# mLSTM head 3: a written instruction order for its backward recursion, later masks and output gate, and one root stage for heads 2 and 3

## The chip, the cores and the metric

The kernel runs on one NeuronCore of a Trainium2 chip. TensorE (PE) does the matrix products, VectorE (DVE), ScalarE (ACT) and GpSimd (POOL) the elementwise work, and SyncE (SP) issues the DMA transfers. The metric is the device time of one launch in microseconds, lower is better; the median of several runs is compared.

## The reference, cut to what matters

The reference is one layer of a hybrid backbone: a modulated RMSNorm, one input projection, a bidirectional mLSTM with 4 heads of 128 channels beside a windowed attention, an output projection with a gated residual, and a convolutional GLU. The part that the change touches is the mLSTM of the last head and the merge behind it:

```python
def step(carry, inp):                       # one chunk of the recursion
    c_st, n_st, m_st = carry
    c_l, n_l, m_l, bt = inp
    m_new = jnp.maximum(bt + m_st, m_l)
    a = jnp.exp(bt + m_st - m_new)
    s = jnp.exp(m_l - m_new)
    return (a * c_st + s * c_l, a * n_st + s * n_l, m_new), (c_st, n_st, m_st)
...
def mlstm_merge(h, o, gain):
    hn = h * lax.rsqrt(jnp.mean(h * h, axis=-1, keepdims=True) + EPS)
    hn = hn.transpose(0, 2, 1, 3).reshape(b, l, MLSTM_W) * gain
    return (hn * jax.nn.sigmoid(o)).astype(o.dtype)
```

The recursion runs once forward and once backward over the chunks. Within a chunk a decay matrix with a triangular mask weights the products of queries and keys. The sum of both directions is divided by its root mean square over the head's channels, multiplied by a gain and by a sigmoid of the gate `o`.

## The kernel before, in words

The sequence of 1024 latent tokens and 256 context tokens is cut in chunks of 128 (8 latent, 2 context). The heads are worked one after the other. While head h runs its recursion, PE also computes dense projections that belong to something else: for heads 0 to 2 the keys, queries, values and gates of head h+1; for head 3 the attention queries (`qgen`, 16 projections `px` in groups of six matmuls with 256 columns each, which VectorE rotates by L319 and L320). The loop at the end of the head section takes one step of `mlstm(h)` and then as many pieces of the dense work as a rate (`RATE3` = 0.37 us a step for head 3) allows. The steps of `mlstm` are numbered n here:

- n = 0 and 1: PE transposes the first two chunks of keys (L653, into PSUM tile `pn`), ScalarE makes the two weighted copies `kwb` (L657) and `kwf` (L659).
- n = 2 to 10: the backward recursion, i = 0 to 8. Each step transposes the keys of two chunks ahead, multiplies (L680), and VectorE adds the product to the decayed state (L688 for the first, L690 after that). In the same steps stand: the loads of the decay matrices `ee` (L647, first three steps), one step of the finish of the head before (`fins`), `mask(i - 2)` (L663, VectorE), `decay` of a chunk (L667, two exponentials on ScalarE), and at i = 7 the output gate (L703 Tanh on ScalarE over 128x1024, L704 on VectorE).
- n = 11 and 12: two steps of the forward recursion over the context chunks (L710, L713, L715), with the last mask and two decays.
- n = 13 to 29: the latent chunks. `first` multiplies queries and keys (L722) and takes a forward step (L710), and VectorE weights the product with the decay (L725). `second` makes the outputs (L733, L734, L736), ScalarE and VectorE combine and divide them (L739 to L748), and L751 sums the squares in `hss`. `decay(5)` to `decay(7)` are in this part.
- finish: a root of `hss` (L784), a reciprocal (L785) and eight products of hidden value, reciprocal and gate, one for a chunk (L787). For heads 0 to 2 this is spread over the recursion of the next head; for head 3 it comes at once at the end.

What sets the order of instructions: inside a `manual_schedule` block, the engines named there run their instructions in the order in which they are written. For the other engines a planner orders them, from its own cost estimates, by what it takes to be ready and by how early they are written. For heads 0 to 2, PE, VectorE, ScalarE, GpSimd and SyncE are all in written order. For head 3 PE alone is; VectorE, ScalarE and SyncE are planned. The instructions of two blocks, or of a block and of the planned code around it, can interleave on an engine.

`pn`, `pe`, `pj`, `pi` and the transposes of the attention queries share four PSUM buffers (pool `pl`), so the transpose of step i waits until VectorE has read the product of the step four tiles before. [...]

At n = 12 (`LW3`) the loop calls `late()`: it loads the second half of the query weights in two DMA transfers through one buffer, and casts and splits each (L156 ScalarE, L157 VectorE). After head 3 the memory of the mLSTM is released, and tiles for the attention (`wm`: `kT2`, `vv`, rows of the output weight) are placed there. The table of Exp is then brought in by L1032. The attention stage and the GLU stage behind it are in written order on PE, VectorE, ScalarE and GpSimd.

Of the kernel before, what the change touches and what calls it, by code (L numbers as in the profile page):

```python
# [12 lines left out]
AF = mybir.ActivationFunctionType  # L13
ALU = mybir.AluOpType
# [4 lines left out]
P = 128  # L19
# [4 lines left out]
NL = SEQ // P  # L24
NC = CTX // P
NCH = NL + NC
H = 4
# [21 lines left out]
TN = 7  # L49
# [29 lines left out]
def build(tc, I, out, dbg=None):  # L79
# [550 lines left out]
        if h == 0:  # L630
            dump("kT", kT[:]); dump("qT", qT[:]); dump("va", va[:].rearrange("p c e -> p (c e)"))

    fins = []

    def mlstm(h, kT, qT, va):
        cbk = tp.tile([P, NL, DH + 1], F32, name="cbk", tag="cbk", bufs=1)
        kwf = tp.tile([P, NCH - 1, DH], F32, name="kwf", tag="kwf", bufs=1)
        hid = tp.tile([P, NL, DH], F32, name="hid", tag="hid", bufs=1)
        hss = tp.tile([P, NL], F32, name="hss", tag="hss")
        g1 = lambda t, d, c: t[:, d, c, h:h + 1]  # L640
        yv = ym[:, :, h * DH:(h + 1) * DH]
        E1 = DH + 1


        ee = tp.tile([P, NL, 2, P], F32, name="ee", tag="ee", bufs=1)
        def ee_load(b):
            nc.sync.dma_start(ee[:, b:b + 2], m_d[:].rearrange("(c h) d t -> h c d t", h=H)  # L647
                              [h:h + 1, NC + b:NC + b + 2].broadcast_to([P, 2, 2, P]))

        ee_load(0)  # L650
        def tr(c):
            pn = pl.tile([P, 512], F32, name="pn", tag="l")
            T.transpose(pn[:, 0:P], kT[:, c * P:(c + 1) * P], ident[:])  # L653
            kwb = None
            if c != NC:
                kwb = tp.tile([P, DH], F32, name="kwb", tag="kwb", bufs=3)
                S.activation(kwb[:], pn[:, 0:P], AF.Copy, scale=g1(gw, 1, c))  # L657
            if c < NCH - 1:
                S.activation(kwf[:, c], pn[:, 0:P], AF.Copy, scale=g1(gw, 0, c))  # L659
            return pn, kwb  # L660

        def mask(b):
            V.tensor_tensor(out=ee[:, b], in0=ee[:, b], in1=tri[:], op=ALU.add)  # L663

        def decay(b):
            for d in range(2):
                S.activation(ee[:, b, d], ee[:, b, d], AF.Exp, bias=g1(a_, d, NC + b), scale=-1.0)  # L667

        ahead = [tr(order[1][0])]
        yield  # L670
        ahead.append(tr(order[1][1]))
        yield
        prev = None
        for i, c in enumerate(order[1][:-1]):
            pn, kwb = ahead.pop(0)
            if i + 2 < NCH - 1:
                ahead.append(tr(order[1][i + 2]))
            elif i + 2 == NCH - 1:
                tr(order[1][i + 2])
            T.matmul(pn[:, P:P + E1], kwb[:], va[:, c], start=True, stop=True)  # L680
            if c == 1:
                nx = tp.tile([P, E1], F32, name="cst", tag="cst")[:]
            elif c == 0:
                nx = cbk[:, NL - 1]
            else:
                nx = cbk[:, c - NC - 1]
            if prev is None:
                V.tensor_copy(nx, pn[:, P:P + E1])  # L688
            else:
                V.scalar_tensor_tensor(out=nx, in0=prev, scalar=g1(gd, 1, c), in1=pn[:, P:P + E1],  # L690
                                       op0=ALU.mult, op1=ALU.add)
            prev = nx
            if i < 3:
                ee_load(2 * i + 2)
            if fins and i:
                next(fins[0])
            if i > 1:
                mask(i - 2)
            if i in (4, 6, 8):
                decay(i // 2 - 2)  # L700
            if i == TN:

                S.activation(yv, yv, AF.Tanh, scale=0.5)  # L703
                V.scalar_tensor_tensor(out=yv, in0=yv, scalar=1.0, in1=rwc("gain", h * DH, DH).unsqueeze(1)  # L704
                                       .broadcast_to([P, NL, DH]), op0=ALU.add, op1=ALU.mult)
            yield
        cf, cfs = [None], []

        def step(c, ps):
            T.matmul(ps, kwf[:, c], va[:, c], start=True, stop=True)  # L710
            nx = tp.tile([P, E1], F32, name="cst", tag="cst")
            if cf[0] is None:
                V.tensor_copy(nx[:], ps)  # L713
            else:
                V.scalar_tensor_tensor(out=nx[:], in0=cf[0], scalar=g1(gd, 0, c), in1=ps, op0=ALU.mult, op1=ALU.add)  # L715
            cf[0] = nx[:]
            cfs.append(nx[:])

        def first(c):
            b = c - NC  # L720
            pe = pl.tile([P, 512], F32, name="pe", tag="l")
            T.matmul(pe[:, 0:P], kT[:, c * P:(c + 1) * P], qT[:, b * P:(b + 1) * P], start=True, stop=True)  # L722
            if b:
                step(c - 1, pe[:, P:P + E1])
            V.scalar_tensor_tensor(out=ee[:, b], in0=pe[:, 0:P].unsqueeze(1).broadcast_to([P, 2, P]),  # L725
                                   scalar=float(DH) ** -0.5, in1=ee[:, b], op0=ALU.mult, op1=ALU.mult)

        def second(c):
            b = c - NC
            qs = qT[:, b * P:(b + 1) * P]  # L730
            pj = pl.tile([P, 512], F32, name="pj", tag="l")
            pi = pl.tile([P, 512], F32, name="pi", tag="l")
            T.matmul(pj[:, 0:E1], qs, cfs.pop(0), start=True, stop=True)  # L733
            T.matmul(pj[:, E1:2 * E1], qs, cbk[:, b], start=True, stop=True)  # L734
            for d in range(2):
                T.matmul(pi[:, d * E1:(d + 1) * E1], ee[:, b, d], va[:, c], start=True, stop=True)  # L736
            nm = tp.tile([P, 2, E1], F32, name="nm", tag="nm")
            for d in range(2):
                S.activation(nm[:, d], pj[:, d * E1:(d + 1) * E1], AF.Copy, scale=g1(gi, d, c))  # L739
            V.tensor_tensor(out=nm[:], in0=pi[:, 0:2 * E1].rearrange("p (d e) -> p d e", d=2), in1=nm[:], op=ALU.add)  # L740
            dn = tp.tile([P, 2], F32, name="dn", tag="dn")
            V.scalar_tensor_tensor(out=dn[:], in0=nm[:, :, DH], scalar=-1.0, in1=nm[:, :, DH], op0=ALU.mult, op1=ALU.max)
            V.tensor_tensor(out=dn[:], in0=dn[:], in1=gfl[:, :, c, h], op=ALU.max)
            V.reciprocal(dn[:], dn[:])

            def rest():
                S.activation(hid[:, b], nm[:, 0, 0:DH], AF.Copy, scale=dn[:, 0:1])
                V.scalar_tensor_tensor(out=hid[:, b], in0=nm[:, 1, 0:DH], scalar=dn[:, 1:2], in1=hid[:, b],  # L748
                                       op0=ALU.mult, op1=ALU.add)
                yield  # L750
                S.activation(nm[:, 0, 0:DH], hid[:, b], AF.Square, accum_out=hss[:, b:b + 1])  # L751
                yield
            return rest()

        for c in range(NC):
            pn = pl.tile([P, 512], F32, name="pn", tag="l")
            step(c, pn[:, 0:E1])
            if c == 0:
                cfs.clear()
            if c == 0:  # L760
                mask(NL - 1)
            decay(3 + c)
            yield
        first(NC)
        tail = None
        yield
        for c in range(NC, NCH):
            if c + 1 < NCH:
                first(c + 1)
            if tail:  # L770
                next(tail)
            yield
            if c < NC + 3:
                decay(5 + c - NC)
            if tail:
                next(tail)
            tail = second(c)
            yield
        for _ in tail:
            pass  # L780
        cfs.clear()

        def finish():
            S.activation(hss[:], hss[:], AF.Sqrt, bias=eps_t[:], scale=1.0 / DH)  # L784
            V.reciprocal(hss[:], hss[:])  # L785
            for b in range(NL):
                V.scalar_tensor_tensor(out=yv[:, b], in0=hid[:, b], scalar=hss[:, b:b + 1], in1=yv[:, b],  # L787
                                       op0=ALU.mult, op1=ALU.mult)
                if b < NL - 1:
                    yield  # L790
            fins.clear()
            yield
        if h < H - 1:
            fins.append(finish())
        else:
            for _ in finish():
                pass

    def ada_second():
        R4 = 4 * KT
# [172 lines left out]
    for h in range(H):  # L977
# [20 lines left out]
        with tc.manual_schedule(engines=order_):  # L998
            dn = dense(h + 1, wkq, wvo, *nh) if nh else qgen()
            rate = RATE if nh else RATE3  # L1000
            for n, _ in enumerate(mlstm(h, *cur)):
                if nh is None and n == LW3:
                    late()
                    rga = pq.tile([P, D], F32, name="rga", tag="rga")
                    nc.sync.dma_start(rga[:], row(0))
# [1177 lines left out]
```

## Time and profile before

| | us |
|---|---|
| median of 3 runs | 1265.78 (1265.62 to 1266.16) |
| time of the profiled execution | 1265.89 |
| its span (first to last instruction) | 1264.1 |
| head 3: first transpose to last product of the last chunk | 322.2 to 354.2 |
| first score of the attention stage | 394.5 |

The granted TensorE clock is 0.998 of full speed. In the profile, a row of a timeline gives start, length, engine, line, operation and tiles, and in brackets the idle time of the engine before it with what ended it. A row of windows gives the busy time of each engine in a stretch with the number of its instructions. A row of the waits gives the engine and line that waited, for whom, the total, the number of times and the longest.

### The profile page before, as it was taken

What the parts mean: (1) busy time and instruction counts of PE and PEld (TensorE: products, weight loads), DVE (VectorE), ACT (ScalarE), POOL (GpSimd) and SP (SyncE); (2) the same over time, 40 slices, a digit from 0 to 9 for tenths busy, and PEclk for the clock granted to TensorE, in tenths of its full rate; (3) what the DMA queues carried; (4) which work ended last, traced back from release to release, by engine and by line L of the source; (5) the groups of instructions that cost most, each with busy time, mean ns of one, the idle gap of its engine ahead of it and who ended that gap; (6) DMA issues with size and microseconds to landing.
All of it is one profiled execution on the core that took longest, in us unless ns stands there. A gap on an engine that the chain in (4) does not pass through costs nothing.

```text
span 1264.1 us, 19253 instructions
## 1 busy us (share of the span) xinstructions
PE 1234.4 (98%) x7047; PEld 1060.2 (84%) x7047; DVE 972.8 (77%) x1691; ACT 637.9 (50%) x1309; POOL 187.1 (15%) x162
## 2 busy tenths in 40 slices
PE   6999999999999999999999999999999999999997
PEld 4799999999898888888887888888888888788886
DVE  5873777777787888788987877777777777877887
ACT  6632556464865777776843333333333334434435
POOL 1200000000001443221002232133231232001000
PEclk9999999999999999999999999999999999999999
DMA  9541535362354333104313322223322237975553
GB/s 361 184 142 34 145 115 153 115 181 75 85 175 160 134 120 115 51 34 167 117 51 130 115 99 102 95 102 117 103 105 100 93 135 269 335 250 187 195 192 134
DMA packets 90560, 176.17 MB, mean 139 GB/s; under 512 B 12954, under 2 KB 29538, under 8 KB 90466
## 3 DMA queue, kind: packets, MB, share of 16 engines
q1 hardware_dynamic: 90178, 174.15, 41.2%
q8 instruction: 56, 0.92, 0.3%
q10 hardware_dynamic: 288, 0.79, 0.2%
q14 instruction: 38, 0.31, 0.1%
HBM read 136.58 MB, written 38.33 MB: 138 GB/s over the span
## 4 chain that ended last, share of the span: by engine, by line
PE 84%; DVE 6%; ACT 5%; DMA 3%; issue 2%; POOL 1%; SPq 0%; ACTq 0%; DVEq 0%; POOLq 0%
PE pd L2020 14%; PE pa L1480 8%; PE pc L1480 8%; PE pp L588 7%; PE pe L1480 4%; PE pd L1480 4%; PE pb L1480 4%; PE u L1182 3%; PE pv L307 2%; PE pv L309 2%; PE pv L308 2%; PE po L307 2%; PE po L309 2%; PE po L308 2%; PE pt L1159 2%
## 5 line engine op out<-in xcount | busy, mean ns | idle before, releaser
L1597 ACT CAST wh<-Rb 128x1024 fp32r<-128x1024 f32 (+1 forms) x63 | 56.8, 903 | 144.1 <-PE pd L1480 77.1
L2020 PE MATMUL pd<-dh,al 128*128 128x512 f32 x296 | 115.4, 390 | 0.9 <-DVE al L1361 0.9
L2020 PE MATMUL pd<-dl,ah 128*128 128x512 f32 x296 | 115.3, 389 | 0.0
L2020 PE MATMUL pd<-dh,ah 128*128 128x512 f32 x296 | 115.1, 389 | 0.0
L1480 PE MATMUL pc<-hB,wh 128*128 128x512 f32 x344 | 105.6, 389 | 0.0
L1480 PE MATMUL pa<-hB,wh 128*128 128x512 f32 x336 | 103.8, 390 | 0.2 <-ACT sn L1679 0.2
L1198 DVE TENSOR_TENSOR wl<-Rb,wh 128x1024 fp32r<-128x1024 f32 (+1 forms) x63 | 65.8, 1045 | 39.2 <-ACT wh L1597 38.6
L1715 POOL TENSOR_TENSOR tt<-vt,tt 128x512 f32<-128x512 f32 x22 | 29.5, 1341 | 367.5 <-ACT tt L1709 367.5
L588 PE MATMUL pp<-hl,wh 128*128 128x512 f32 x256 | 79.3, 405 | 0.0
L307 PE MATMUL pv<-wh,hl 128*128 128x256 f32 x256 | 75.9, 296 | 0.0
L1480 PEld LDWEIGHTS pc<-hB,wh 128*128 128x128 f32 x344 | 64.6, 188 | 13.5
L1480 PEld LDWEIGHTS pa<-hB,wh 128*128 128x128 f32 x336 | 62.9, 188 | 14.1 <-ACT sn L1679 1.1
L309 PE MATMUL pv<-wh,hl 128*128 128x256 f32 x256 | 72.4, 283 | 0.0
L308 PE MATMUL pv<-wl,hl 128*128 128x256 f32 x256 | 72.3, 282 | 0.0
L2020 PEld LDWEIGHTS pd<-dh,al 128*128 128x128 f32 x296 | 55.6, 188 | 13.1 <-DVE al L1361 1.6
L1480 PE MATMUL pc<-hB,wl 128*128 128x512 f32 x172 | 66.4, 389 | 0.0
L2020 PEld LDWEIGHTS pd<-dl,ah 128*128 128x128 f32 x296 | 55.5, 188 | 11.8 <-DVE dl L1361 0.3
L1480 PE MATMUL pa<-hB,wl 128*128 128x512 f32 x168 | 65.4, 389 | 0.0
L2020 PEld LDWEIGHTS pd<-dh,ah 128*128 128x128 f32 x296 | 55.6, 188 | 11.6
L1166 ACT CAST ph<-pt 128x512 fp32r<-128x512 f32 (+1 forms) x88 | 46.2, 525 | 25.3 <-PE pt L1159 25.0
L1136 DVE TENSOR_REDUCE nm<-sps 128x1 f32<-128x641 f32 (+1 forms) x64 | 50.3, 786 | 4.9 <-PE sps L1132 3.4
L1480 PE MATMUL pd<-hB,wh 128*128 128x512 f32 x176 | 54.0, 390 | 0.0
(1082 smaller groups left out, 3694.4 us busy)
## 6 DMA issues: line engine op xcount, KB each, us to landing
w<-in_w_ada_dram SPq DMA_DIRECT2D x64, 256.0 KB, 2.8
br<-in_w_down_dram SPq DMA_DIRECT2D x25, 512.0 KB, 5.9
ar<-act_s SPq DMA_DIRECT2D x44, 256.0 KB, 4.0
Ra<-in_w_up_dram SPq DMA_DIRECT2D x21, 512.0 KB, 3.6
Rb<-in_w_up_dram SPq DMA_DIRECT2D x21, 512.0 KB, 3.6
act_a<-tt SPq DMA_DIRECT2D x33, 256.0 KB, 2.0
act_s<-tt SPq DMA_DIRECT2D x33, 256.0 KB, 2.0
wr<-in_w_h_dram SPq DMA_DIRECT2D x16, 512.0 KB, 4.1
```

The costliest lines, as they stand in the source:

```text
L307: T.matmul(ps, st_hi, mv_hi, start=first, stop=False)
L308: T.matmul(ps, st_hi, mv_lo, start=False, stop=False)
L309: T.matmul(ps, st_lo, mv_hi, start=False, stop=last)
L588: T.matmul(pp[:, 512 * n:512 * n + 512], wkq[sw][:, kt, cs], hl[n][part][:, kt, :], start=kt == 0 and sw + part == 0, stop=kt == KT - 1 an ...
L1136: V.tensor_reduce(out=self.nm[:, j:j + 1], in_=self.sv[j], axis=AX.X, op=ALU.max, negate=True)
L1166: S.copy(self.ph[i][:, :w], self.pt[i][:, :w])
L1182: T.matmul(self.u[:], vv[:, c, self.g], part[i][:, kk * 2 * P:(kk + 1) * 2 * P], start=kb + m == 0, stop=kb == last and m == 1)
L1198: sub = lambda e, o, x, y: e.tensor_tensor(out=o, in0=x, in1=y, op=ALU.subtract)
L1480: T.matmul(ps[:, cols], wt[sw][:, j, kt * P:kt * P + P], hB[part][:, blk, kt, cols], start=first and n == 0, stop=last and n == len(seq) - ...
L1597: S.copy(wt[0][:], src)
L1715: G.tensor_tensor(out=self.tt[:, h2_], in0=self.vt[:], in1=self.tt[:, h2_], op=ALU.mult)
L2020: T.matmul(ps[:], ac[sa][:, js], w[sw], start=first and n == 0, stop=last and n == 2, skip_group_check=not fresh)
```

## The change

Seven edits, all for the mLSTM:

1. For head 3, VectorE, ScalarE and GpSimd too are put in written order, from the start of head 3 to n = 13; the block is left there. SyncE stays planned.
2. `late_` = 2 for head 3: in the backward recursion, `mask(i - 4)` takes the place of `mask(i - 2)`, so five masks and two decays are there in place of seven and three. The other masks and decays follow one by one at n = 11, 12 and 13; `decay(5)` to `decay(7)` stay where they were.
3. The output gate of head 3 leaves step i = 7 and comes behind the squares of chunk b = 2, in the second half of the head (n = 21), where the planner orders.
4. The finish of head 2, inside head 3's recursion, is one product of 128x1024 (hidden value by gate) at i = 1 in place of a root, a reciprocal and eight products. It needs no root.
5. At the end of head 3: one such product for head 3, then two roots, then two reciprocals, then two products of 128x1024 with the reciprocal broadcast along the channels (heads 2 and 3).
6. The Sqrt table is thus brought in once for heads 2 and 3, at the end.
7. `late()` moves from n = 12 to n = 13, behind the end of the block.

```diff
-            if i > 1:
-                mask(i - 2)
-            if i in (4, 6, 8):
-                decay(i // 2 - 2)
-            if i == TN:
-
-                S.activation(yv, yv, AF.Tanh, scale=0.5)
-                V.scalar_tensor_tensor(out=yv, in0=yv, scalar=1.0, in1=rwc("gain", h * DH, DH)...
+            if i > 1 + late_:
+                mask(i - 2 - late_)
+            if i in (4 + late_, 6 + late_, 8):
+                decay((i - late_) // 2 - 2)
+            if i == TN and not late_:
+                gate()
...
                 S.activation(nm[:, 0, 0:DH], hid[:, b], AF.Square, accum_out=hss[:, b:b + 1])
+                if late_ and b == 2:
+                    gate()
...
-            if c == 0:
-                mask(NL - 1)
-            decay(3 + c)
+            if late_:
+                mask(5 + c)
+                decay(2 + c)
+            else:
+                if c == 0:
+                    mask(NL - 1)
+                decay(3 + c)
             yield
         first(NC)
+        if late_:
+            mask(NL - 1)
+            decay(4)
...
+        def gated():
+            V.tensor_tensor(out=yv, in0=hid[:], in1=yv, op=ALU.mult)
+            held.append((hss, yv))
+            fins.clear()
+            yield
-        if h < H - 1:
+        if h < H - 2:
             fins.append(finish())
+        elif h < H - 1:
+            fins.append(gated())
         else:
-            for _ in finish():
+            for _ in gated():
                 pass
+            for s_, _ in held:
+                S.activation(s_[:], s_[:], AF.Sqrt, bias=eps_t[:], scale=1.0 / DH)
+            for s_, _ in held:
+                V.reciprocal(s_[:], s_[:])
+            for s_, y_ in held:
+                V.tensor_tensor(out=y_, in0=y_, in1=s_[:].unsqueeze(2).broadcast_to([P, NL, DH]), op=ALU.mult)
...
+            if nh is None:
+                inner = tc.manual_schedule(engines={mybir.EngineType.DVE, mybir.EngineType.Activation, mybir.EngineType.Pool})
+                inner.__enter__()
             for n, _ in enumerate(mlstm(h, *cur)):
-                if nh is None and n == LW3:
+                if nh is None and n == LW3 + 1:
+                    inner.__exit__(None, None, None)
                     late()
```

`gate()` is a new function that holds the two instructions removed above (L703 and L704).

More of the change, by code (lines that the diff above doesn't have):

```diff
@@ L631, in dense @@
             dump("kT", kT[:]); dump("qT", qT[:]); dump("va", va[:].rearrange("p c e -> p (c e)"))
-    fins = []
+    fins, held = [], []
     def mlstm(h, kT, qT, va):
@@ L667, in decay, with gate @@
                 S.activation(ee[:, b, d], ee[:, b, d], AF.Exp, bias=g1(a_, d, NC + b), scale=-1.0)
+        def gate():
+            S.activation(yv, yv, AF.Tanh, scale=0.5)
+            V.scalar_tensor_tensor(out=yv, in0=yv, scalar=1.0, in1=rwc("gain", h * DH, DH).unsqueeze(1)
+                                   .broadcast_to([P, NL, DH]), op0=ALU.add, op1=ALU.mult)
+        late_ = 2 if h == H - 1 else 0
         ahead = [tr(order[1][0])]
@@ L696, in mlstm @@
                 next(fins[0])
-            if i > 1:
-                mask(i - 2)
-            if i in (4, 6, 8):
-                decay(i // 2 - 2)
-            if i == TN:
-                S.activation(yv, yv, AF.Tanh, scale=0.5)
-                V.scalar_tensor_tensor(out=yv, in0=yv, scalar=1.0, in1=rwc("gain", h * DH, DH).unsqueeze(1)
-                                       .broadcast_to([P, NL, DH]), op0=ALU.add, op1=ALU.mult)
+            if i > 1 + late_:
[4 more added lines that the diff above has]
+                gate()
             yield
```

## The prediction

> **What bounds the kernel now.** The order of reading was: the page for the span, the windows over head 3 for where PE loses time, the waits for what ended its idle time, the timeline of PE, and last the groups of VectorE and ScalarE in the stretch where PE waits.
>
> ```profile
> span 1264.1 us, 19253 instructions
> ```
>
> The profiled execution took 1265.89 us, 1.8 us more than this span, and lies 0.11 us over the median of 1265.78 us. The sum below is made against 1265.89.
>
> The windows give, from left, PE, weight loads, VectorE, ScalarE and GpSimd:
>
> ```profile
> 325.00:330.00 5.00, 3.85 (x29) 3.10 (x27) 4.43 (x13) 4.26 (x13) 0.00 (x0) 1.00 0.96 173
> 330.00:335.00 5.00, 4.19 (x33) 3.61 (x32) 5.00 (x19) 4.97 (x16) 0.00 (x0) 1.00 0.20 70
> 335.00:340.00 5.00, 5.00 (x46) 5.00 (x46) 4.96 (x14) 4.75 (x15) 0.00 (x0) 1.00 0.18 59
> 340.00:345.00 5.00, 5.00 (x46) 5.00 (x45) 4.53 (x17) 3.43 (x11) 0.00 (x0) 1.00 0.15 54
> 345.00:350.00 5.00, 4.21 (x37) 4.05 (x36) 4.74 (x23) 3.39 (x14) 0.00 (x0) 1.00 0.26 102
> 350.00:355.00 5.00, 5.00 (x46) 5.00 (x46) 3.76 (x17) 4.18 (x15) 0.00 (x0) 1.00 0.14 52
> ```
>
> Between 325 and 335 PE starts 62 matmuls, against 46 in five microseconds where it runs full. VectorE and ScalarE are nearly full there, so they are what PE waits for. The second thing to see is VectorE at 4.5 to 5.0 of 5 until 350: behind the recursion there is little room on it.
>
> ```profile
> PE pj L733 <- DVE ee L725: 0.8, 1, 0.8
> PE pn L653 <- DVE cst L688: 0.7, 1, 0.7
> ...
> PE pn L680 <- ACT kwf L659: 0.6, 2, 0.4
> ```
>
> These are PE's largest waits in head 3. Busy time understates the loss, because the end of a pipelined matmul is modelled; the starts show it better:
>
> ```profile
> 324.89 0.27 PE L653 MATMUL pn<-ident,kT 128*128 128x128 f32 x1
> 325.36 0.49 PE L680 MATMUL pn<-va,kwb 128*128 128x129 f32 x2 [0.20 <-ACT kwf L659]
> 326.57 0.33 PE L653 MATMUL pn<-ident,kT 128*128 128x128 f32 x1 [0.73 <-DVE cst L688]
> ...
> 327.68 0.28 PE L653 MATMUL pn<-ident,kT 128*128 128x128 f32 x1
> 327.79 0.39 PE L680 MATMUL pn<-va,kwb 128*128 128x129 f32 x2
> 327.93 0.36 PE L307 MATMUL px<-wh,hl 128*128 128x256 f32 x1
> ...
> 333.88 0.39 PE L710 MATMUL pn<-va,kwf 128*128 128x129 f32 x2
> ...
> 335.76 0.61 PE L722 MATMUL pe<-qT,kT 128*128 128x128 f32 x4
> ```
>
> The stretch from the transpose of step n = 3 (324.89) to the first forward step (333.88) takes 8.99 us. Unhindered, a transpose takes 0.11 us from start to start (327.68 to 327.79), a product 0.14 (327.79 to 327.93), and two forward steps, each a product and a group of six projection matmuls, 1.88 (333.88 to 335.76), which leaves 0.80 for a group. Steps n = 3 to 10 hold seven transposes, eight products and four groups: 0.77 + 1.12 + 3.20 = 5.09 us. PE loses **3.9 us** here. That is the most that this stretch can give.
>
> **What VectorE and ScalarE do meanwhile,** from 323.9 to 335.8, first VectorE, then ScalarE:
>
> ```profile
> L663 DVE TENSOR_TENSOR ee<-ee,tri 128x256 f32<-128x256 f32 x8 | 3.2, 420 | 1.6 <-DMA ee<-m_d 1.6
> L787 DVE SCALAR_TENSOR_TENSOR ym<-hid,hss,ym 128x128 f32<-128x128 f32 x8 | 2.6, 347 | 0.0
> L690 DVE SCALAR_TENSOR_TENSOR cbk<-cbk,gd,pn 128x129 f32<-128x129 f32 x7 | 2.4, 339 | 0.0
> L704 DVE SCALAR_TENSOR_TENSOR ym<-ym,rw 128x1024 f32<-128x1024 f32 x1 | 1.2, 1220 | 0.0
> ```
>
> ```profile
> L657 ACT ACTIVATE kwb<-pn,gw 128x128 f32<-128x128 f32 x8 | 2.7, 356 | 0.7 <-PE pn L653 0.7
> L784 ACT ACT_TABLE_LOAD x1 | 1.3, 1283 | 0.0
> L667 ACT ACT_TABLE_LOAD x1 | 1.3, 1283 | 0.0
> L156 ACT CAST wh<-wr 128x1024 fp32r<-128x1024 f32 x1 | 1.1, 1052 | 0.0
> L703 ACT ACTIVATE ym<-ym 128x1024 f32<-128x1024 f32 x1 | 1.0, 1044 | 0.0
> ```
>
> Only the L690 row (and L688) is the recursion itself. The masks stood idle 1.6 us for their DMA in front of the first state, which is the 0.7 us wait on L688 above.
>
> **The recursion after the change.** Removed from VectorE: eight products (2.6 us), the gate (1.2), three of eight masks, which come after the backward steps, and the idle 1.6 us, since the first mask now stands at n = 6. Added: one product of 128x1024, which the trace does not have in this form; the nearest row is L704, 1.22 us. What is left in n = 3 to 10 is eight states, four masks in front of the last state, three rotations of a projection (of the kind of the masks, 0.42) and that product. By durations: 8 x 0.34 + 4 x 0.42 + 3 x 0.42 + 1.22 = 6.9 us. But one instruction starts before the last has ended: the window 330 to 335 has 19 of them in 5.00 us, 0.26 each, so the lower end is 15 x 0.26 + 1.22 = 5.1 us, which is also PE's own bound. I take the middle, **6.1 us** in place of 8.99, a gain of **2.9** (2.1 to 3.9). ScalarE loses two table loads (2.57 us), the gate (1.04) and one decay; 16 weighted copies, at most 0.36 each, and two exponentials are some 6 us by durations and less by starts, so it doesn't set a later end. Written order means that the copies are never behind a table load again.
>
> [...]
>
> **The latent chunks (n = 13 to 29).** The gate now comes here: 1.22 us of VectorE, 1.04 of ScalarE. The same number of masks and decays stands before n = 13 but one mask. In return a rotation and the scaling of a query half, 0.42 each, which were late on VectorE, are done when the chunks begin. So VectorE has up to 1.2 us more, at best 0.4 more, in a stretch in which it idles 0.77 us between 335 and 350 and 1.24 from 350 to 355. PE in turn has its 0.8 us wait at L733, which could go. The cost lies between -0.8 and +1.2; I take **0.2**, near the hidden end, because ScalarE has 1.6 us free in each of the windows from 340 to 350 and the planner may place the gate's two instructions in any gap. If that cover is gone it is 1.2.
>
> **The end of head 3.**
>
> ```profile
> 353.62 0.61 PE L736 MATMUL pi<-va,ee 128*128 128x129 f32 x4
> ...
> 362.37 1.28 ACT L1032 ACT_TABLE_LOAD   x1 [2.13 <-DVE ym L787]
> ...
> 394.53 0.35 PE L1125 MATMUL sps<-kT,QT 128*128 128x256 f32 x1
> ```
>
> One root, one reciprocal and two products of about 1.2 us stand where eight of 0.35 stood; the product of hidden value and gate (1.2) runs while ScalarE loads the table. So the tiles of the attention are released, and their DMAs start, up to 0.5 us later against PE's work. PE has projections until the first score at 394.5, which hide it: I take 0.1, up to 0.5 if the rows of the output weight then come late. `late()` moves one step back; its weights are used by the fifth projection, near n = 27.
>
> **The sum:** 2.9 - 0.2 - 0.1 = 2.6 us. 1265.89 - 2.6 = 1263.3, on the median 1265.78 - 2.6 = **1263.2 us**. From the ends: 2.1 - 1.2 - 0.5 = 0.4 to 3.9 + 0.8 = 4.7, so 1261.1 to 1265.4. The stages behind are written in order and bound by PE, so they are only shifted.
>
> **Rivals.** (1) VectorE takes the gain back in the latent chunks. For it: 4.96, 4.53 and 4.74 of 5 us, with PE full beside it, so a PE that comes 2.9 us early finds VectorE at its old pace plus the gate. Against: the eight products and the 1.6 us idle are gone before. Then the gain is 0.4 to 1.4: 1264.9 us.
>
> (2) Slower: a cast of `late()` is put too early. The planner may place foreign instructions between those in written order; it did so with the gate, written at n = 9:
>
> ```profile
> 323.46 1.04 ACT L703 ACTIVATE ym<-ym 128x1024 f32<-128x1024 f32 x1
> ...
> 326.84 0.35 SPq L152 DMA_DIRECT2D wr<-in_w_q_dram  x1
> ```
>
> ```profile
> wr<-in_w_q_dram SPq DMA_DIRECT2D x2, 512.0 KB, 4.8
> ```
>
> The weights land 4.8 us after 326.84, at 331.6. If ScalarE, now with gaps in the planner's estimate, has the L156 cast in its queue at 326 to 328, it stands 4 to 5.6 us, the copies of all later steps are queued behind, and PE waits for them. Less the 2.6 won that is 1.4 to 3 us slower, 1267.2 to 1268.8. It decides from a place more than 2.6 us before the landing, 329.0. Against: the cast now is written later than before, when it ran 4 us after landing.
>
> (3) The change doesn't do what it says: PE's waits are the latency of transpose, two copies, product and state, whatever stands between. By the rows 0.33 + 2 x 0.36 + 0.39 + 0.34 = 1.8 us for a chain of which two are always in flight: 8 x 0.9 = 7.2 us, a gain of 1.8 less 0.3: 1264.3 us.
>
> **How the numbers follow.** A measurement of this kernel can tell 0.2%, 2.5 us, from no change. Forecast 0.60: faster by more than that 0.47, within it 0.13. Rival 1: 0.19, all within. Rival 2: 0.15, slower by more than that 0.09, within it 0.06. Rival 3: 0.06, within. That is 0.47 faster, 0.44 same, 0.09 slower. The forecast's own range is 1261.1 to 1265.4. The range given reaches from 1261.6, near its end, to 1266.0, past rivals 1 and 3 and short of 2.
>
> **What would show it.** The stretch from the transpose at n = 3 to the first L710 of the forward recursion should take 6.1 us (5.1 to 6.9) with no table load and no L787 in it; the L733 wait of 0.8 should be 0.3 to 1.5; from the first L722 to the last L736 17.9 us now, 17.1 to 19.1 then; from there to the first score 40.9 us, unchanged to 0.5. The forecast is wrong if the first stretch is over 7.5 us, if L156 stands in ScalarE's order ahead of a weighted copy, or if the second stretch grows by more than 1.2.

## The result

The changed kernel takes 1270.39 us in the median of seven runs (1269.10 to 1272.19), the kernel before 1266.16 us beside it (1265.62 to 1267.48): a ratio of 1.0029 with a 95% interval of 1.0020 to 1.0038. It is **slower by 4.2 us**. Forecast were 1263.2 us, with 0.09 for slower. Rival 2, the cast that is put too early, is what happened.

The profiled execution took 1270.49 us. From its page:

```profile
span 1268.7 us, 19241 instructions
```

The windows over head 3 of the changed kernel, with the columns PE, weight loads, VectorE, ScalarE, GpSimd, granted TensorE clock, DMA share and GB/s, first three as quoted of before, then two of one microsecond:

```profile
325.00:330.00 5.00, 4.48 (x35) 4.24 (x36) 4.81 (x13) 4.58 (x14) 0.00 (x0) 1.00 0.87 182
330.00:335.00 5.00, 1.90 (x14) 1.70 (x13) 1.44 (x5) 2.30 (x4) 0.00 (x0) 0.93 0.13 51
335.00:340.00 5.00, 5.00 (x33) 4.89 (x32) 3.93 (x10) 4.73 (x15) 0.00 (x0) 0.73 0.00 0
```

```profile
335.00:336.00 1.00, 1.00 (x7) 1.00 (x7) 0.86 (x4) 0.99 (x3) 0.00 (x0) 0.50 0.00 0
336.00:337.00 1.00, 1.00 (x7) 1.00 (x6) 0.36 (x2) 1.00 (x5) 0.00 (x0) 0.50 0.00 0
```

Until 330 PE does better than before (35 matmuls in place of 29): this is the gain that was forecast. Then everything stands: 14 matmuls between 330 and 335, and VectorE and ScalarE are busy for 1.44 and 2.30 us of the five. And from 335 to 340 PE shows as fully busy but starts 33 matmuls in place of 46, with a granted clock of 0.50 in both of the short windows. That second loss can't be seen in busy time at all.

VectorE's groups from 323.9 to 335.8 show what the change did there, and where the time went instead (the last figures are the idle time ahead of the group):

```profile
L696 DVE SCALAR_TENSOR_TENSOR cbk<-cbk,gd,pn 128x129 f32<-128x129 f32 x7 | 2.4, 345 | 3.8 <-PE pn L686 3.7
L663 DVE TENSOR_TENSOR ee<-ee,tri 128x256 f32<-128x256 f32 x5 | 2.1, 418 | 0.0
L807 DVE TENSOR_TENSOR ym<-hid,ym 128x1024 f32<-128x1024 f32 x1 | 1.2, 1219 | 0.0
L671 DVE SCALAR_TENSOR_TENSOR ym<-ym,rw 128x1024 f32<-128x1024 f32 x1 | 1.2, 1215 | 0.0
```

Five masks stand for eight, none waits for its DMA, and one product (1.22 us, as forecast) stands for the eight of the old finish; but the states waited 3.7 us for PE. The last row is the gate's product (L671). It was to leave the recursion and is still here.

PE's largest waits from 318 to 400 (the second of them lies behind head 3, at 384.64):

```profile
PE pn L686 <- ACT kwf L659: 3.7, 3, 3.1
PE pt L905 <- DVE qs L900: 1.2, 1, 1.2
PE pi L739 <- DVE ee L728: 0.7, 1, 0.7
```

ScalarE's timeline of the changed kernel tells what `kwf` waited for, and the one row of SyncE's queue when it was fetched:

```profile
323.23 1.04 ACT L670 ACTIVATE ym<-ym 128x1024 f32<-128x1024 f32 x1
...
326.47 1.28 ACT L819 ACT_TABLE_LOAD   x1
...
329.22 0.39 ACT L659 ACTIVATE kwf<-pn,gw 128x128 f32<-128x128 f32 x1
332.68 1.04 ACT L156 CAST wh<-wr 128x1024 fp32r<-128x1024 f32 x1 [3.07 <-DMA wr<-in_w_q_dram]
333.63 0.36 ACT L657 ACTIVATE kwb<-pn,gw 128x128 f32<-128x128 f32 x1
333.89 0.36 ACT L659 ACTIVATE kwf<-pn,gw 128x128 f32<-128x128 f32 x1
334.27 1.28 ACT L667 ACT_TABLE_LOAD   x1
```

```profile
327.11 0.35 SPq L152 DMA_DIRECT2D wr<-in_w_q_dram  x1
```

The transfer was issued at 327.11; the cast of `late()` stood at the head of ScalarE's queue from 329.6 and waited 3.07 us for it. The key copies of the next step (333.63, 333.89) were ready to go and stood behind. In the kernel before, the same cast comes after all copies of the recursion:

```profile
335.56 1.05 ACT L156 CAST wh<-wr 128x1024 fp32r<-128x1024 f32 x1
```

The first row of ScalarE's timeline is the gate's Tanh. It is written at n = 21, outside the block, and the planner put it where it stands in the kernel before (323.46 there); its product on VectorE follows at 324.35. What came into the latent chunks in its place is a product that the change writes at the end of head 3, the product of head 2 with its reciprocal, since head 2's root was taken early (load at 326.47):

```profile
343.17 1.21 DVE L823 TENSOR_TENSOR ym<-ym,hss 128x1024 f32<-128x1024 f32 x1
```

PE's timeline of the changed kernel, for the landmarks and the clock:

```profile
324.66 0.27 PE L653 MATMUL pn<-ident,kT 128*128 128x128 f32 x1
...
330.93 0.28 PE L309 MATMUL px<-wh,hl 128*128 128x256 f32 x1
334.31 0.80 PE L686 MATMUL pn<-va,kwb 128*128 128x129 f32 x2 [3.10 <-ACT kwf L659]
334.90 0.64 PE L713 MATMUL pn<-va,kwf 128*128 128x129 f32 x2
...
335.76 0.41 PE L309 MATMUL px<-wh,hl 128*128 128x256 f32 x1
335.97 0.41 PE L307 MATMUL px<-wh,hl 128*128 128x256 f32 x1
...
338.07 0.61 PE L725 MATMUL pe<-qT,kT 128*128 128x128 f32 x4
...
338.99 0.29 PE L309 MATMUL px<-wh,hl 128*128 128x256 f32 x1
339.11 0.28 PE L307 MATMUL px<-wh,hl 128*128 128x256 f32 x1
...
357.23 0.61 PE L739 MATMUL pi<-va,ee 128*128 128x129 f32 x4
...
398.65 0.35 PE L1151 MATMUL sps<-kT,QT 128*128 128x256 f32 x1
```

The recursion's stretch now ends at 334.90, 10.24 us after the transpose of n = 3. The two forward steps behind it (334.90 to 338.07) take 3.17 us in place of 1.88, with the same instructions: from start to start 0.21 us (335.76 to 335.97) where the full clock gives 0.12 (338.99 to 339.11).

All kernels of this study read by the same landmarks, in us. "Chunks" is from the first product of queries and keys to the start of the last matmul of the last L739 group (0.3 us behind the group's row), "longest PE wait" is that from 318 to 400, "clock" the lowest granted clock of a one-microsecond window in the same stretch. Stages and waits are those of the one profiled execution, median and ratio those of all runs; each ratio is against runs of the kernel before that were taken beside it (medians 1266.16 to 1266.53):

| kernel | recursion | two forward steps | chunks | to the first score | longest PE wait | clock | median | ratio (95%) |
|---|---|---|---|---|---|---|---|---|
| before | 9.00 | 1.88 | 18.19 | 40.58 | 0.8 | 1.00 | 1266.16 | |
| after | 10.24 | 3.17 | 19.49 | 41.09 | 3.1 | 0.50 | 1270.39 | 1.0029 (1.0020 to 1.0038) |
| a_late_in | 6.61 | 1.88 | 19.48 | 41.22 | 1.2 | 1.00 | 1265.38 | 0.9992 (0.9983 to 1.0001) |
| b_one_root | 10.67 | 3.21 | 19.08 | 40.33 | 3.6 | 0.50 | 1270.17 | 1.0030 (1.0019 to 1.0041) |
| c_both | 6.56 | 1.88 | 18.75 | 41.06 | 1.3 | 1.00 | 1264.99 | 0.9988 (0.9979 to 0.9996) |
| d_planned | 6.13 | 1.87 | 18.63 | 40.65 | 0.7 | 1.00 | 1264.06 | 0.9980 (0.9971 to 0.9989) |
| e_early_load | 11.24 | 3.23 | 18.24 | 41.09 | 3.1 | 0.50 | 1269.81 | 1.0027 (1.0017 to 1.0037) |
| f_planned_one_root | 6.14 | 1.87 | 19.23 | 41.45 | 1.2 | 1.00 | 1265.53 | 0.9990 (0.9981 to 0.9999) |
| g_only_order | 10.01 | 1.87 | 19.85 | 40.38 | 1.2 | 1.00 | 1269.21 | 1.0023 (1.0014 to 1.0032) |
| h_only_later | 8.13 | 1.88 | 18.97 | 41.52 | 1.2 | 1.00 | 1267.39 | 1.0006 (0.9997 to 1.0015) |
| i_only_roots | 5.99 | 1.88 | 21.47 | 40.88 | 2.3 | 0.50 | 1267.04 | 1.0003 (0.9994 to 1.0012) |
| j_order_late_in | 8.51 | 1.92 | 19.90 | 40.91 | 1.2 | 1.00 | 1268.20 | 1.0014 (1.0005 to 1.0023) |
| k_no_load | 8.61 | 1.87 | 18.13 | 40.98 | 1.1 | 1.00 | 1266.17 | 1.0000 (0.9991 to 1.0009) |
| l_roots_later | 6.40 | 1.87 | 18.85 | 40.19 | 0.6 | 1.00 | 1264.00 | 0.9982 (0.9973 to 0.9991) |

From before to after the spans differ by 4.6 us: 1.24 in the recursion, 1.29 in the two forward steps, 1.30 in the chunks, 0.51 in the projections up to the first score, about 0.5 behind it, less 0.2 ahead of it.

### The profile page after: what moved, and what is told of

The parts are those of the page before. It is cut to its first block, busy times and chain, and to the rows that moved or that the text cites. A ratio compares the mean times of both kernels' runs of the same rounds, so it can differ in the third digit from the quotient of the medians.

```text
span 1268.7 us, 19241 instructions
## 1 busy us (share of the span) xinstructions
PE 1235.7 (97%) x7047; PEld 1061.6 (84%) x7047; DVE 974.4 (77%) x1679; ACT 638.4 (50%) x1309; POOL 187.7 (15%) x162
## 4 chain that ended last, share of the span: by engine, by line
PE 81%; DVE 7%; ACT 6%; DMA 3%; issue 2%; POOL 1%; SPq 0%; ACTq 0%; DVEq 0%; POOLq 0%
PE pd L2046 14%; PE pa L1506 9%; PE pc L1506 9%; PE pp L588 7%; PE pe L1506 5%; PE pd L1506 4%; PE pb L1506 4%; PE pv L307 2%; PE pv L309 2%; PE pv L308 2%; PE u L1208 2%; PE pt L1185 2%; PE px L309 2%; PE px L307 2%; PE px L308 2%
```

## The experiments

**Is it the cast?** `late()` and the row load behind it are written inside the block, so that the cast keeps its place behind the copies written before it. Nothing else differs from after.

```diff
-                    inner.__exit__(None, None, None)
                     late()
                     rga = pq.tile([P, D], F32, name="rga", tag="rga")
                     nc.sync.dma_start(rga[:], row(0))
+                    inner.__exit__(None, None, None)
```

> The changed kernel with one edit: late() is called before the written-order block is left, so the cast of the query weights stands behind the decays of the backward recursion on ScalarE. Theory 1 (ScalarE stands 3.1 us for the weights' DMA in front of a cast that the planner put between two key copies): that wait goes, the stretch from the transpose at n = 3 to the first forward step falls from 10.2 to about 7 us, and the kernel loses 3 us against the changed one, to about +1 us over the kernel before. Theory 2 (the masks, decays and gate that were moved back overload VectorE in the chunks): the 10.2 may fall, but the stretches behind grow by as much, and the kernel stays at +4 us.

ScalarE's timeline of a_late_in:

```profile
330.96 0.36 ACT L659 ACTIVATE kwf<-pn,gw 128x128 f32<-128x128 f32 x1
331.33 1.28 ACT L667 ACT_TABLE_LOAD   x1
...
336.12 1.04 ACT L156 CAST wh<-wr 128x1024 fp32r<-128x1024 f32 x1
```

The cast comes behind the copies and waits for nothing; the recursion falls from 10.24 to 6.61 us, the clock stays at 1.00, and the kernel gains 5.0 us on after (about +1 us over the kernel before was expected, it came to 1.0 under). That settles the cause of the slowdown: it was the place of this one instruction among the copies; the gate and the table loads keep the places that they have in after (323.88, 327.12 and 331.33). The kernel is still not clearly faster than before: in its trace, 2.39 us are won in the recursion, 1.29 lost in the chunks, which take 19.48 us as they do in after, and 0.64 lost behind them. This profiled execution took 1266.31 us, 0.9 more than the median, so one of its stages may read too long.

**Is it the table loads?** The root of head 2 was brought forward by the planner into the recursion (326.47 above), since each head had a tile of its own for its sums of squares. Here both share one tile, so that a single root stands at the end.

```diff
+        if h == H - 2:
+            both.append(tp.tile([P, 2, NL], F32, name="hss2", tag="hss2", bufs=1))
+        hss = both[0][:, h - H + 2] if both else tp.tile([P, NL], F32, name="hss", tag="hss")
...
-            for s_, _ in held:
-                S.activation(s_[:], s_[:], AF.Sqrt, bias=eps_t[:], scale=1.0 / DH)
-            for s_, _ in held:
-                V.reciprocal(s_[:], s_[:])
+            S.activation(both[0][:], both[0][:], AF.Sqrt, bias=eps_t[:], scale=1.0 / DH)
+            V.reciprocal(both[0][:], both[0][:])
```

> The changed kernel with one edit: the square sums of heads 2 and 3 lie in one tile and get one Sqrt and one reciprocal at the end, so the root of head 2 can't be taken early. In the changed kernel it was taken inside the recursion, with two table loads (1.28 us each). Theory 1: the cast still stands ahead of the last key copies and the DMA lands at the same time, so ScalarE waits as long or longer (3 to 5 us) and the kernel stays at +3 to +4 us. A theory that the two table loads are the cost expects 2.6 us less, about +1.5 us.

> Both edits of the two kernels before: the cast behind the recursion, one root for both heads. Nothing foreign but the gate is left in the recursion. Theory 1: the stretch from the transpose at n = 3 to the first forward step takes 5.5 to 6.5 us in place of 10.2 (9.0 in the kernel before), and the kernel comes to 1 to 3 us under the kernel before. Theory 2: VectorE gives all of it back in the chunks; the same time as before, or up to 1 us over.

ScalarE of b_one_root:

```profile
333.77 1.04 ACT L156 CAST wh<-wr 128x1024 fp32r<-128x1024 f32 x1 [4.09 <-DMA wr<-in_w_q_dram]
```

Both loads are gone from the recursion (the two at the end, at 361.7 and 366.1, were there in after too), and the cast, reached earlier, waits 4.09 us in place of 3.07. The kernel is where after is. With the cast in its place (c_both against a_late_in) taking the loads out leaves the recursion at 6.56 against 6.61 us and the medians 0.4 us apart, inside both intervals. So the 2.6 us of loading cost nothing that can be measured here.

**Is it the wait or the work?** In k_no_load both casts of `late()` read keys that are already there, and these weights aren't fetched; the casts may still be placed early.

```diff
-            nc.sync.dma_start(raws[q][:, :, :w], src[:, 4 * q:4 * q + 4, :])
+            if fetch:
+                nc.sync.dma_start(raws[q][:, :, :w], src[:, 4 * q:4 * q + 4, :])
...
-            late = lambda: wq.append(load_split(..., lambda: pq.tile([P, 4, 256], F32, name="wr", tag="rga")))
+            late = lambda: wq.append(load_split(..., lambda: cur[0][:, 0:4 * 256].rearrange("p (k f) -> p k f", k=4), fetch=False))
```

> The changed kernel without the load of the second half of the query weights: both casts read 1024 columns of the keys of head 3, which are there, so nothing of these two transfers is waited for (the attention queries of that half are not those of the reference). One cast is placed ahead of the recursion, one still between key copies. Theory 1: ScalarE stands nowhere for a DMA, the stretch from n = 3 to the first forward step is 7 to 8.5 us in place of 10.2 (the two table loads and a cast of 1.04 stay in it), and the kernel comes to 2 to 5 us under the changed one. If the cast's place among the copies is the cost by itself, it stays within 1 us of the changed one.

It is 4.2 us under after with a clock of 1.00 throughout. Its recursion is still 8.61 us against 6.61 of a_late_in, and PE's largest wait tells why:

```profile
PE pn L654 <- DVE cbk L697: 2.0, 2, 1.1
```

Both subtractions of `late()` (324.89 and 327.95) and the gate's product (330.02), 1.22 us each, stand on VectorE between the states. So work that is moved in there costs about 2 us, which mostly returns in the chunks (18.13 against 19.48); the wait and the clock behind it are what after loses. An earlier start of the transfer should do the same. In after the transfer can't start before `row_d` has been written from `arw` (issued at 322.78; SyncE's queue waits 2.7 us for it), whose buffer is in its way; here `arw` is elsewhere:

```diff
-            arw = ap2.tile([P, 512], F32, name="arw", tag="w20")
+            arw = xp.tile([P, 2 * P], F32, name="arw", tag="kv", bufs=3)
```

> The changed kernel with one edit: the small tile `arw` (the rows written to row_d) lies in the buffers of `kv`, not in the memory that the attention's buffers take over, so the load of the query weights need not wait for the DMA that reads it and can start some 4 us earlier. The cast stays ahead of the last key copies in ScalarE's order. Theory 1 (the price is the wait for the landing, not the cast's 1.04 us nor its place): ScalarE's idle time at the cast falls from 3.1 us to under 1, and the kernel comes down by 2 to 3.5 us from the changed one, to within 2 us of the kernel before. A theory that the cast's place or length is the cost expects no change.

This missed. ScalarE's timeline and SyncE's queue of e_early_load:

```profile
323.29 1.05 ACT L156 CAST wh<-wr 128x1024 fp32r<-128x1024 f32 x1
...
333.79 1.04 ACT L156 CAST wh<-wr 128x1024 fp32r<-128x1024 f32 x1 [3.15 <-DMA wr<-in_w_q_dram]
```

```profile
319.35 0.33 SPq L152 DMA_DIRECT2D wr<-in_w_q_dram  x1
...
324.60 0.98 SPq L875 DMA_DIRECT2D kb<-kv_d  x2
325.68 0.41 SPq L152 DMA_DIRECT2D wr<-in_w_q_dram  x1
326.13 3.59 SPq L875 DMA_DIRECT2D kb<-kv_d  x4
```

The first half was there at 323.29, but then the planner put the cast of the second half into the same place. That half was issued at 325.68, between six loads of keys that also could start earlier, and its cast could begin 8.1 us later. The wait moved from one half to the other: 3.15 us, PE's wait 3.1, the clock 0.50. By its time alone this run fits the rival theory, which expected no change; that the wait is the price rests on k_no_load.

**What is each part of the change worth?** First the change without the written order of three engines:

```diff
-            if nh is None:
-                inner = tc.manual_schedule(engines={mybir.EngineType.DVE, mybir.EngineType.Activation, mybir.EngineType.Pool})
-                inner.__enter__()
...
-                    inner.__exit__(None, None, None)
```

> The changed kernel without the written-order block: VectorE, ScalarE and GpSimd are ordered by the planner for all of head 3 as before; masks, gate, root and the place of late() are as in the change. Theory 1: no cast ahead of the key copies (it stands behind the decays), so no 3 us wait; about the kernel before, within 1 us. Theory 2 (the moved work is the cost): still +3 to +4 us.

It is **faster than before**, 1264.06 us with a ratio of 0.9980 (0.9971 to 0.9989), where the same time within 1 us was expected, and its waits from 318 to 400 are small:

```profile
PE pt L905 <- DVE qs L900: 0.7, 1, 0.7
...
PE pn L686 <- ACT kwf L659: 0.2, 1, 0.2
```

Then, each on the kernel before, only the block (with `late()` behind it), only the later masks and gate, and only the merged finish; and the block with `late()` inside it. The first of them:

```diff
+            if nh is None:
+                inner = tc.manual_schedule(engines={mybir.EngineType.DVE, mybir.EngineType.Activation, mybir.EngineType.Pool})
+                inner.__enter__()
             for n, _ in enumerate(mlstm(h, *cur)):
-                if nh is None and n == LW3:
+                if nh is None and n == LW3 + 1:
+                    inner.__exit__(None, None, None)
                     late()
```

> The kernel before with the written-order block and the later late() alone; masks, gate, decays and the finish stay as before. Theory 1: the cast again stands ahead of the last key copies and waits for its DMA, so the kernel is 2 to 5 us over the kernel before. Theory 2 (the later masks and gate are the cost): no slower than the kernel before.

> The kernel before with the written-order block, late() called inside it: the kernel with the block alone (2.9 us over the kernel before, stretch 10.0 us) but for the cast's place behind the recursion. Theory 1 (the wait of the cast is the price of the block): the stretch falls by 2 us (1.0 us of idle ScalarE and the cast's 1.0) to about 8, and the kernel comes to 0.5 to 1.5 us over the kernel before. If the written order itself, with the masks in front of the states on VectorE, is the larger part, the stretch stays over 9 us and the kernel over 2 us.

g_only_order is slower, 1.0023. PE's waits in it:

```profile
PE pn L653 <- DVE cbk L690: 2.2, 4, 0.8
PE pn L680 <- ACT kwf L659: 1.2, 1, 1.2
PE pi L736 <- DVE ee L725: 1.2, 1, 1.2
```

With the cast kept behind (j_order_late_in) the wait for `kwf` is gone, but the 2.2 us for `cbk` and the 1.2 for `ee` stay, and it remains slower than before, 1.0014; the two intervals overlap. Its stretch of 8.51 us and its 1.7 us over the kernel before lie between what the two theories had. Written order thus has a price of its own with the old finish. It doesn't show in the recursion, which is 0.5 us shorter than before's, but in the chunks (19.90 against 18.19 us). VectorE's timeline of j_order_late_in shows part of it:

```profile
327.31 0.20 DVE L785 RECIPROCAL hss<-hss 128x8 f32<-128x8 f32 x1 [1.65 <-ACT hss L784]
327.54 0.35 DVE L787 SCALAR_TENSOR_TENSOR ym<-hid,hss,ym 128x128 f32<-128x128 f32 x1
327.81 0.34 DVE L690 SCALAR_TENSOR_TENSOR cbk<-cbk,gd,pn 128x129 f32<-128x129 f32 x1
```

VectorE waits 1.65 us for head 2's root with a state behind it whose product PE had started at 326.27, and it comes to the first L725 at 338.50, where before's stands at 336.18. That this delay is the whole price is argued and not shown: no run leaves out the old finish and nothing else.

The later masks and gate alone are items 2 and 3 of the change, with the lines that its diff has for them, and planned; the merged finish alone is this:

```diff
-        if h < H - 1:
+        if h < H - 2:
             fins.append(finish())
+        elif h < H - 1:
+            fins.append(gated())
         else:
-            for _ in finish():
+            for _ in gated():
                 pass
+            for s_, _ in held:
+                S.activation(s_[:], s_[:], AF.Sqrt, bias=eps_t[:], scale=1.0 / DH)
...
```

> The kernel before with the later masks and gate alone: no written-order block, the finish of heads 2 and 3 as before, late() at n = 12 as before. Theory 1: the cast stands behind the decays; the stretch from the transpose at n = 3 to the first forward step is shorter than 9.0 us because the masks no longer stand in front of the first state, about 7.5 us, but the table loads and eight products stay; 0 to 1.5 us under the kernel before. Theory 2: 1 us or more over it.

> The kernel before with the merged finish alone: one product for head 2 inside the recursion of head 3, the roots of heads 2 and 3 at the end; order, masks, gate and late() as before. If the gain of the planned kernel (2.35 us under the kernel before, its stretch 6.1 us) is that of the shorter finish, the stretch from the transpose at n = 3 to the first forward step is 6.1 to 7 us and the kernel is 1.5 to 2.5 us under the kernel before; if it needs the later masks too, the stretch is 7.5 us or more and the kernel within 1 us.

Neither differs measurably from before (1.0006 and 1.0003), where up to 1.5 and 1.5 to 2.5 us of gain had been expected. In h_only_later the planner left the gate's product at 327.46 (327.48 before), so in effect it has the later masks and decays alone. And i_only_roots has the shortest recursion of all, 5.99 us, but loses its gain in the chunks. Its rows of PE, VectorE, ScalarE and one window:

```profile
337.25 0.92 PE L736 MATMUL pi<-va,ee 128*128 128x129 f32 x4 [2.34 <-DVE ee L725]
```

```profile
334.30 1.23 DVE L157 TENSOR_TENSOR wl<-wr,wh 128x1024 fp32r<-128x1024 f32 x1 [1.27 <-ACT wh L156]
...
336.78 0.42 DVE L725 SCALAR_TENSOR_TENSOR ee<-pe,ee 128x256 f32<-128x256 f32 x1
```

```profile
333.22 1.05 ACT L156 CAST wh<-wr 128x1024 fp32r<-128x1024 f32 x1 [1.15 <-DMA wr<-in_w_q_dram]
```

```profile
339.00:340.00 1.00, 1.00 (x7) 1.00 (x6) 1.00 (x7) 0.87 (x1) 0.00 (x0) 0.50 0.00 0
```

It is the same fault on another engine. The copies being done earlier, the cast waits 1.15 us for the weights; the subtraction L157 on VectorE waits 1.27 us for the cast; and a rotation and the first products L725 stand behind it, which PE needs for L736. PE waits 2.34 us, and the clock drops to 0.50. Whether that is the whole loss was tested by writing `late()` five steps later, at n = 17:

```diff
-                if nh is None and n == LW3:
+                if nh is None and n == LW3 + 5:
```

> The kernel before with only the merged finish (as i_only_roots), and `late()` written five steps later, at n = 17, so that in VectorE's order the subtraction L157 stands behind the first two L725 products instead of ahead of a rotation and of all of them, and in ScalarE's order the cast L156 stands behind the first query half. Theory (what the merged finish wins in the recursion was lost in the chunks to the late weights, on VectorE): recursion stretch 6.0 us as in i_only_roots, from the first L722 to the last L736 18.2 to 19.2 us in place of 21.5, and the 2.34 us wait of L736 for L725 under 0.8; the kernel 1.5 to 3 us under before, ratio 0.9976 to 0.9988. Rival (the chunks lose it whatever stands in front of L725, since VectorE is full there): the chunks stay at 20.5 to 21.5 us and the ratio at 0.9995 to 1.001.

VectorE's timeline of l_roots_later:

```profile
335.05 0.41 DVE L725 SCALAR_TENSOR_TENSOR ee<-pe,ee 128x256 f32<-128x256 f32 x1
335.38 1.21 DVE L157 TENSOR_TENSOR wl<-wr,wh 128x1024 fp32r<-128x1024 f32 x1
```

The subtraction now stands behind two of the products and waits for nothing. The chunks fall from 21.47 to 18.85 us, the wait for L725 is gone, and the kernel is at 1264.00 us, 0.9982 (0.9973 to 0.9991): with the merged finish and a later `late()` alone, it is as fast as d_planned, and both are faster than before and after.

Last, d_planned with the single root of b_one_root (both diffs above together):

> The changed kernel without the written-order block and with one root for heads 2 and 3 in one tile. If the two table loads that the early root of head 2 brings into the chunks still cost PE, this is faster than the planned kernel with two roots (2.35 us under the kernel before) by up to 1 us; if they are hidden there, it is the same within 0.5 us.

The expectation missed: its median is 1.5 us over d_planned's, with 19.23 us in the chunks against 18.63 and 41.45 us behind them against 40.65. The two intervals overlap (0.9981 to 0.9999 and 0.9971 to 0.9989), so that it is slower is likely but not sure. In d_planned the planner brought head 2's root forward to 336.8, into the chunks. What makes the difference was not settled.

## Why the prediction was wrong

**The step that failed** is what the prediction said of ScalarE: "it doesn't set a later end", and "Written order means that the copies are never behind a table load again". ScalarE did set the end. The block binds what is written in it. What is written outside, head 2's root, the gate and the cast of `late()`, was still placed by the planner: the table loads that the root brought stood between the copies, at 326.47 and 334.27, and so did the cast, at 332.68. Of these the cast cost time, as a_late_in and c_both show: 3.07 us of waiting on ScalarE, 3.10 on PE, and a recursion of 10.24 us in place of 6.1. The prediction knew the danger, since rival 2 says that the planner may place foreign instructions there, and quotes the gate as a case. It then argued against the rival that "the cast now is written later than before, when it ran 4 us after landing". That was the weak argument: when an instruction is written says little once it isn't bound to the order, and the 4 us of margin were the recursion's slowness, which the change was to remove. An earlier end of the copies brings the cast to the head of ScalarE's queue before its data is there; i_only_roots shows that with no written order at all. All three of the prediction's signs of being wrong came: the long stretch, the cast ahead of copies, and 1.30 us more in the chunks.

**The recursion: right in size, in part by luck, and not in this kernel.** The forecast of 6.1 us (5.1 to 6.9, whose middle is 6.0) is what every kernel with the merged finish shows whose casts stay away: 6.13 in d_planned, 5.99 in i_only_roots, 6.61 in a_late_in. But the sum took four things off VectorE (the finish's products, the gate, three masks, a wait for a DMA), and the gain comes from the first: i_only_roots reaches 5.99 us with six masks and the gate's product (330.16) still in the stretch, and the later masks alone give 8.13. In after itself the gate's product stands where the stretch begins (324.35).

**Rival 2's price was too low.** Its place for the cast, 326 to 328 with a landing at 331.6, gives a stall of 3.6 to 5.6 us, where it says 4 to 5.6; less 2.6 won that is 1 to 3 us slower. Its condition (a place more than 2.6 us ahead of the landing) was met, with 3.07, which by its rule is 0.5 us slower. Measured between the profiled executions are 4.6. What it lacked is the cast's own work, about 1 us before the next copy can start (332.68 to 333.63), and the clock: the two forward steps behind the stall cost 1.29 us more at a granted clock of 0.50, which no step of the sum had. The chunks add 1.1 us to their forecast, and the stages behind them about 0.9.

**The chunks: mis-sized, and for another reason than the one given.** Forecast was a cost of 0.2 (-0.8 to 1.2) for the gate, which would come here. Measured are 1.30 in after, 1.29 in a_late_in and 0.44 in d_planned. But in after and in a_late_in the gate stands ahead of the chunks; what came into them is head 2's product with its reciprocal (343.17 and 347.11), 1.2 us as well, and one or two masks. In b_one_root and c_both, where that product stands at the end, the chunks cost 0.89 and 0.56. Yet d_planned has the gate's product among them (338.31), with head 2's only at their very end (351.70), and pays 0.44, so one such product doesn't always cost 1.3. The runs don't show what sets the cost. Before n = 13 there is also a decay less, which the prediction didn't count.

**The end and the rest.** The forecast of 0.1 was for two roots, reciprocals and products at the end. d_planned meets it with 0.07 up to the first score, but by luck: its planner had taken head 2's root and product forward (336.81 and 351.70). With all of it at the end and one root, the change against before is -0.25 in b_one_root, 0.48 in c_both and 0.87 in f_planned_one_root; in after it is 0.51. The whole sum of 2.6 us is 2.35 in d_planned, which has no written order. That one table load would do for heads 2 and 3 was not so as built (326.47 and 361.69 in after), and as c_both shows it doesn't matter measurably.

Rival 1 is not what made after slow. It may be part of what a_late_in loses: VectorE is busy for 18.34 of 19.40 us of its chunks; no run separates it. In i_only_roots the gain was lost in its place, VectorE in the chunks, but by a wait and not by being full. Rival 3 falls: with 6.0 to 6.6 us the latency of a step can't be 0.9 us for each of eight.

## What to carry to other kernels

A block of written order doesn't keep other instructions out, so whatever a planner may still place there, above all a cast or a subtraction that waits for a DMA, must be written inside the block behind the work it may not delay, or late enough that its data has landed. Before a stretch is made shorter, look up which instructions behind it were covered by its slowness, and price the stall at what is queued behind them. And price a wait of PE with the clock behind it: after the waits of 2.34 to 3.6 us here the granted clock was 0.50 for some 3.4 us, and two forward steps in after took 1.29 us longer. Read the granted clock by microsecond, since busy time hides it (1.00 of 1.00 us from 336 to 337 in after, at 0.50).

## What the runs showed of the hardware

**After PE waits of 2.34 to 3.6 us the granted clock was 0.50.** It was so after the waits of 2.34 us in i_only_roots, 3.1 us in after and in e_early_load, and 3.6 us in b_one_root, while in the kernels whose longest wait from 318 to 400 was 1.3 us or less it stayed at 1.00; nothing between 1.3 and 2.34 was measured. In after it was 0.50 from 334.3 to 337.7, some 3.4 us, in which PE starts a matmul every 0.21 us in place of 0.12. In i_only_roots the 3.4 us run from 337.6 to 341.0, so they began 0.3 us after PE had started again (337.25). The runs don't show what sets these times.

**A table load took 1.28 us.** In after the root of head 2 has one ahead of it (326.47) and the exponentials behind it another (334.27). The root starts at 327.76 and the first of these exponentials at 335.57, each 1.3 us after its load had begun.

**The landing of the same 512 KB varied.** For the weights of `late()` the kernel before shows 4.8 us in the median. From the issue to the start of the cast that waited for it, it was 5.6 us in after (327.11 to 332.68) and 8.1 in e_early_load (325.68 to 333.79), where loads of keys were issued around it. The prediction's rival 2 put the landing at 331.6, by the median.
